# A block of activations split in two halves, modulation sums dealt to other places, and first loads asked for earlier in a two-layer denoising network on one core

## Chip, core and metric

The kernel runs on one core of a Trainium2 chip. The metric is the device time of one execution in microseconds (us). The engines are called by the names of the profile: PE (TensorE, matmuls; PEld is its weight load), DVE (VectorE), ACT (ScalarE), POOL (GpSimd) and SP (SyncE, which here only issues DMAs).

## What is computed

Two layers work on a latent stream of 256 tokens and a context stream of 256 tokens, D = 1024 features each. A layer is a gated FFN, a mixer (layer 0: a short convolution; layer 1: attention) and a second FFN. Each is entered through a modulated norm and left through a modulated gate. The shift, the scale and the gate of each are modulations: nine vectors of 1024 per layer, a product of a conditioning vector with a 1024 x 9216 matrix.

```python
mod  = (silu(c) @ mod_w[i] + mod_b[i]).reshape(bsz, 3, 3, 1, D_MODEL)
modc = (silu(c_ctx) @ mod_w[i] + mod_b[i]).reshape(3, 3, D_MODEL)
lat = lat + 0.5 * mod[:, 0, 2] * _swiglu(_modulate(lat, norm_g[i, 0], mod[:, 0, 0], mod[:, 0, 1]), ffn_w13[i, 0], ffn_w2[i, 0])
cx  = cx  + 0.5 * modc[0, 2] * _swiglu(_modulate(cx, norm_g[i, 0], modc[0, 0], modc[0, 1]), ffn_w13[i, 0], ffn_w2[i, 0])
h, hc = _modulate(lat, norm_g[i, 1], ...), _modulate(cx, norm_g[i, 1], ...)
y, yc = mixer(h, hc)                       # convolution in layer 0, attention in layer 1
lat = lat + mod[:, 1, 2] * y
cx  = cx + modc[1, 2] * yc                 # layer 0 only, as the context's second FFN
...
lat = lat + 0.5 * mod[:, 2, 2] * _swiglu(_modulate(lat, norm_g[i, 2], ...), ffn_w13[i, 1], ffn_w2[i, 1])
```

## The kernel before

**Layout.** Activations lie with features on the 128 partitions and tokens in columns: x is 8 blocks (KT) of 128 features by 512 columns, the latent stream (s = 0) in the first 256 columns and the context (s = 1) in the last 256.

**Precision.** Every matmul operand is split into a high and a low part in fp32r, and three products stand for one (lines 136 to 138). `split` is an ACT copy into the high part (line 107) and a DVE subtraction for the low part (line 108). Weights are split on the fly: a raw tile `wr` is loaded by SP (`load_raw`, line 103; 8 buffers), then split into `wh` and `wl`.

**Stages.** The opening (to 44 us), whose order is written out by hand, then the first FFN of layer 0 (44 to 391), the convolution with its output projection (to 566), the second FFN (to 918), the first FFN of layer 1 (to 1249), attention with its output projection (to about 1360), the last FFN. An FFN runs in three thirds of 8, 7 and 7 blocks of hidden features. A third is a row of pairs (the up and the gate weights of a block) followed by a projection back to the 1024 features (`project`).

**Pairs.** Both streams together are treated as a 2 x 2 block product in seven products instead of eight: half of the features by stream on the one side, the weights' halves on the other. `Pair` loads the raws of a pair (r2, then the right half of r1), POOL scales the left half of r2 by -1 (line 709) and adds the rest by an accumulating DMA (line 712), DVE takes further sums (lines 731 and 739), and `head`, `five`, `six`, `seven` and `four` are the products with their evacuations; `head` copies p and `five` copies q (line 762, tile gm) out of PSUM on ACT.

**Norms.** `tail_norm` collects squares at the end of a projection. The last two output blocks are computed for the latent stream first, then for the context, so that the latent's norm is under way while the context's part is still multiplied. `Blocks.block` forms a block of four feature blocks of a stream: t = x * scale * 1/rms on DVE (line 299), then t + shift. For the latent stream (`fine`) each 256 columns go into bh (ACT, line 391) and bl (DVE, line 392) at once and also into a raw `hr`; for the context the four go into `hr` (ACT, line 396) and are then split as one piece of 1024 columns. `Blocks.sums` then forms the sums of the blocks that the pairs need (`hr` lines 417 to 424). There are three such norms: before the convolution (about 372 to 391), before the second FFN (545 to 566) and before layer 1 (895 to 918).

**Modulation sums.** All modulations but the first two are computed on DVE, one sum (`mod_unit`, line 177) for each tile of 128 x 1024 of the transposed matrix and each stream, 224 sums in all. Their raws `modT` go through the same 8 buffers of `wr` and SP's queue as the weights, and one is always loaded ahead. `tick(n)` adds n to an account and does as many whole sums as it then holds; `project` calls it after its first output blocks with `ev`, `ffn` after each pair with 0.9, the convolution with 0.5. The tuple given to `ffn` holds the `ev` of the first two thirds' projections and that of the last. Where a norm or a gate needs a modulation that isn't done (`mod_ready`, `gate_of`), the missing sums are done on the spot:

```python
    def mod_ready(l, ch):
        while not ((l, ch) in done and done[l, ch] == 8 * streams(l, ch)):
            next_unit()
        return modv[l, ch]
```

**The opening.** The first two modulations are sums on PE (`mod_pe`, line 945) over tiles `pm` that SP loads (line 932) behind the four chunks of x (512 KB, two feature blocks each). `first_sums` squares x by chunks; a one-column copy from x into a pm tile (line 995) makes the loads of pm wait until that chunk of x has landed.

Of the kernel before, what the change touches and what calls it, by code (L numbers as in the profile page):

```python
# [9 lines left out]
F32 = mybir.dt.float32  # L10
# [10 lines left out]
T2 = 2 * S  # L21
# [27 lines left out]
def hybrid_kernel(ctx: ExitStack, tc: tile.TileContext, a: dict, out: bass.AP):  # L49
    nc = tc.nc  # L50
# [55 lines left out]
    def split(hi, lo, src):  # L106
        nc.scalar.activation(out=hi, in_=src, func=AF.Copy)  # L107
        return nc.vector.tensor_tensor(out=lo, in0=src, in1=hi.bitcast(F32), op=ALU.subtract)  # L108
# [105 lines left out]
    def tick(n, at=None):  # L214

        place[:] = [at] if at else []
        owed[0] += n
        while (jobs or units) and owed[0] >= 1:
            owed[0] -= 1
            next_unit()  # L220
        place.clear()
# [93 lines left out]
    def hot(s, dt=F32R):  # L315
        return hop.tile([P, 1024], dt, name=nm(s), tag="hop")
# [56 lines left out]
    class Blocks:  # L373
# [5 lines left out]
        def block(self, s, hf, A, B, ri, fine=False, ks=range(4)):  # L379
            if ks[0] == 0:  # L380
                self.raw[hf, s] = hot("hr", F32)
                self.t["B", hf, s] = hot("bh"), hot("bl")
            raw = self.raw[hf, s]
            hi, lo = self.t["B", hf, s]
            for i in ks:
                k = 4 * hf + i
                c = slice(i * S, i * S + S)
                t = scaled(s, k, A, ri)
                b = B[:, k, s : s + 1]
                if fine:  # L390
                    nc.scalar.activation(out=hi[:, c], in_=t, func=AF.Identity, bias=b)
                    nc.vector.scalar_tensor_tensor(
                        out=lo[:, c], in0=t, scalar=b, in1=hi[:, c].bitcast(F32),
                        op0=ALU.add, op1=ALU.subtract,
                    )
                nc.scalar.activation(out=raw[:, c], in_=t, func=AF.Identity, bias=b)
            if not fine:
                split(hi, lo, raw)

        def at(self, k, c0, c1):  # L400
            return self.blk(("B", k // 4, c0 // S), k % 4)
# [411 lines left out]
    def ffn(l, b, h, tot, gate, tail, gs=(), ev=(0, 0), z=None):  # L813
        gs = list(gs)
        i0 = 0
        for t, n in enumerate(THIRDS):
            between = ()
            if tot == T2:
                heads = []
                if t == 0 and not gs:  # L820

                    gs = [new_pair("g") for _ in range(2)]
                    heads.append(opening(
                        h, [a["w13"][l, b, 0], a["w13"][l, b, 1], lambda: Pair(a["w13"][l, b, 2], h)],
                        lambda pp, i: w13_post(pp, gs[i], 0, T2),
                    ))
                prev = None
                for i in range(len(gs), n):
                    if t == 0 and not heads and i in AS_IS[l, b]:
                        w = load_w(a["w13"][l, b, i])  # L830
                        pp = psum("pg"), psum("pu")
                        if prev:
                            prev.seven()
                        if "T1" not in h.t:
                            with tc.issue_after(rows["W1"]):
                                h.sums()
                        w13_mm(pp, w, h, range(4), 0, T2)
                        if prev:
                            gs.append(new_pair("g"))
                            prev.four(gs[-1])  # L840
                            prev = None
                        w13_mm(pp, w, h, range(4, KT), 0, T2)
                        gs.append(new_pair("g"))
                        tick(3, w13_post(pp, gs[-1], 0, T2))
                        continue
                    if heads:
                        pr = heads.pop(0)
                    else:
                        pr = Pair(a["w13"][l, b, i0 + i], h)
                        pr.sums(0)  # L850
                        pr.sums(1)
                        pr.head()
                    pr.five()
                    at = prev.seven().ins if prev else None
                    pr.six()
                    if prev:
                        gs.append(new_pair("g"))
                        prev.four(gs[-1])
                    prev = pr
                    if i:  # L860
                        tick(0.9, at)

                def last():
                    gs.append(new_pair("g"))
                    prev.four(gs[-1])

                between = (prev.seven, last) if prev else ()
            else:
                for i in range(n):
                    w = load_w(a["w13"][l, b, i0 + i])  # L870
                    gs.append(beside(gp.tile([P, T2], F32R, name=nm("gx"), tag="gh")))
                    pp = psum("pg"), psum("pu")
                    if i0 + i < EARLY:
                        for k in range(KT):
                            for j in range(2):
                                ps = pp[j][:, : z.w]
                                mm3(ps, w(at13(1 - j, k)), z.at(k), k == 0, k == KT - 1)
                            if i == 0 and k == KT // 2:
                                flush(1)
                        if i < 3:  # L880
                            flush(1)
                        early_post(pp, gs[i], z.ri)
                        tick(1)
                        continue
                    for j in range(2):
                        ws = [w(at13(1 - j, k)) for k in range(KT)]
                        mm_wide(pp[j], ws, [h.both(k) for k in range(KT)], True, True)
                    beside_post(pp, gs[i])
                    tick(1)
# [78 lines left out]
    def first_sums():  # L968

        pq = psmall("ss")  # L970
        sq = []

        def square(k, eng):
            tag = "gm" if k % 4 < 2 else "sg"
            t = tp.tile([P, T2], F32, name=nm("sq"), tag=tag, bufs=3)
            if eng is nc.vector:
                nc.vector.tensor_tensor(out=t, in0=x[:, k, :], in1=x[:, k, :], op=ALU.mult)
            else:
                nc.scalar.activation(out=t, in_=x[:, k, :], func=AF.Square)
            sq.append(t)  # L980

        def add():
            a, b = sq[-2:]
            nc.vector.tensor_tensor(out=a, in0=a, in1=b, op=ALU.add)
            n = len(sq)
            for i in range(4):
                nc.tensor.matmul(
                    pq[:, i * P : i * P + P], a[:, i * P : i * P + P], ones,
                    start=(n, i) == (2, 0), stop=(n, i) == (KT, 3), skip_group_check=True,
                )  # L990

        square(0, nc.scalar)
        square(1, nc.vector)
        rows[1, 0] = [hot("pm", F32) for _ in range(2)]
        nc.vector.tensor_copy(rows[1, 0][0][:, :1], x[:, 2, :1])
        add()
        square(2, nc.scalar)
        square(3, nc.scalar)
        add()
        nc.scalar.activation(out=sccol[:, :, 2:4], in_=ccol, func=AF.Silu)  # L1000
        square(4, nc.scalar)
        square(5, nc.vector)
        add()
        square(6, nc.scalar)
        square(7, nc.scalar)
        add()
        nc.vector.tensor_scalar(
            out=sb1, in0=modb[:, 0, KT : 2 * KT], scalar1=1.0, scalar2=None, op0=ALU.add
        )
        return pq  # L1010
# [145 lines left out]


    hn = Blocks()
    ffn(0, 0, h, T2, gate_of(0, 0), tail_norm(0, 1, hn), gs0, (4, 3.4))
    h = hn  # L1160

    zs, ds = [], {}
# [52 lines left out]
    for n in range(2, len(parts)):  # L1215
        if n == 2:
            pr = opening(h, [a["cw_cx"][0], a["cw_cx"][1], parts[2]], conv_post)
        else:
            pr = parts[n]()
            pr.sums(0)  # L1220
            pr.sums(1)
            pr.head()
        pr.five()
        at = prev.seven().ins if prev else None
        pr.six()
        if prev:
            prev.four(None)
        prev = pr
        tick(0.5, at)
    between = (prev.seven, lambda: prev.four(None))  # L1230

    def by_pairs(key, box=None):
# [10 lines left out]
    def ws_out(m):  # L1243
# [3 lines left out]
    hn = Blocks()  # L1247
    project(
        ws_out, lambda k, c0, c1: (zs[k][0][:, c0:c1], zs[k][1][:, c0:c1]), KT,
        gate_of(0, 1), tail_norm(0, 2, hn), T2, 2, 4, between,  # L1250
    )
    h = hn
    hn = Blocks()
    ffn(0, 1, h, T2, gate_of(0, 2), tail_norm(1, 0, hn), (), (3.6, 3))
    h = hn


    hn = Plain()
    ffn(1, 0, h, T2, gate_of(1, 0), tail_norm(1, 1, hn), (), (2.8, 2.2))
    h = hn  # L1260
    ap = ctx.enter_context(tc.tile_pool(name="ap", bufs=2))

# [347 lines left out]
```

## Time and profile before

| | us |
|---|---|
| median of 3 runs | 1549.24 (1548.73 to 1550.27) |
| profiled execution | 1548.97 |
| its span | 1547.2 |
| PE busy | 1533.5 |
| DVE busy | 1298.2 |
| ACT busy | 852.2 |
| POOL busy | 301.3 |

The span runs from the first to the last instruction of the profile; the execution's time lies 1.8 us above it. A line of the profile names the source line, the engine, the operation and the tiles by the program's names (out <- in, buffer numbers left out). The time of L107 and L108 is that of all callers of `split`; the tile says which.

### The profile page before, as it was taken

To read this page: it belongs to the slowest core of one execution; us is meant where nothing else is said; L and a number is where in the kernel's file an instruction comes from. 1 tells how busy PE (TensorE), PEld (TensorE's weight loads), DVE (VectorE), ACT (ScalarE), POOL (GpSimd) and SP (SyncE) were. 2 spreads that over 40 slices of the span, in tenths; PEclk is the share of its full clock that TensorE was granted. 3 is DMA by queue.
4 is the path that set the end of the run, shared out by engine and by line. 5 is a ranking of instruction groups with operands and counts; after the bars stand their busy time and mean duration, and the time that the engine had idled before them with its cause. 6 is when DMAs were issued, how large, how long until landed. Compare 5 with 4: busy or idle time off the path is not lost.

```text
span 1547.2 us, 27333 instructions
## 1 busy us (share of the span) xinstructions
PE 1533.5 (99%) x10594; PEld 1423.6 (92%) x10594; DVE 1298.2 (84%) x1964; ACT 852.2 (55%) x1468; POOL 301.3 (19%) x265
## 2 busy tenths in 40 slices
PE   8999999999999999999999999999999999999999
PEld 6898998999999899989999899989999899998888
DVE  5888788898989999968979889958968788998676
ACT  5644554645655376446456466446456456774553
POOL 0013313402231023042052112043042002300000
PEclk9999999999999999999999999999999999999999
DMA  9568768765356636695796625785697743476562
GB/s 377 199 188 235 162 184 232 164 194 143 75 143 175 206 91 151 212 216 135 213 214 153 207 68 136 220 189 138 210 220 182 253 159 114 142 246 220 170 195 76
DMA packets 97474, 278.80 MB, mean 180 GB/s; under 512 B 11456, under 2 KB 13120, under 8 KB 97344
## 3 DMA queue, kind: packets, MB, share of 16 engines
q1 hardware_dynamic: 69408, 228.10, 45.4%
q0 software_dynamic: 25920, 47.20, 18.1%
q10 hardware_dynamic: 2016, 1.76, 0.4%
q8 instruction: 83, 1.36, 0.4%
q14 instruction: 47, 0.39, 0.1%
HBM read 262.07 MB, written 1.05 MB: 170 GB/s over the span
## 4 chain that ended last, share of the span: by engine, by line
PE 89%; DVE 6%; DMA 2%; ACT 1%; issue 1%; POOL 0%; SPq 0%; DVEq 0%; POOLq 0%; ACTq 0%
PE p L138 8%; PE p L137 8%; PE p L136 8%; PE py L137 8%; PE py L136 8%; PE py L138 8%; PE q L138 6%; PE q L136 6%; PE q L137 6%; PE py L144 2%; PE pu L144 2%; PE pg L144 2%; DVE wl L108 1%; DMA wr<-in_w 1%; PE py L146 1%
## 5 line engine op out<-in xcount | busy, mean ns | idle before, releaser
L107 ACT ACTIVATE wh<-wr 128x1024 fp32r<-128x1024 f32 (+2 forms) x454 | 400.5, 909 | 289.2 <-PE py L137 94.5
L108 DVE TENSOR_TENSOR wl<-wr,wh 128x1024 fp32r<-128x1024 f32 (+2 forms) x454 | 468.6, 1056 | 107.0 <-ACT wh L107 87.0
L177 DVE CUSTOM_DVE_ANT_0 junk<-wr,scbc,first 128x1024 bf16<-128x1024 f32 x209 | 269.9, 1291 | 2.2 <-DMA wr<-in_modT 0.2
L137 PE MATMUL py<-gl,wh 128*128 128x512 f32 (+1 forms) x570 | 213.4, 374 | 0.0
L136 PE MATMUL py<-gh,wh 128*128 128x512 f32 (+1 forms) x570 | 213.4, 374 | 0.0
L138 PE MATMUL py<-gh,wl 128*128 128x512 f32 (+1 forms) x570 | 212.8, 373 | 0.0
L709 POOL TENSOR_SCALAR wr<-wr 128x512 f32<-128x512 f32 x66 | 125.4, 1900 | 424.0 <-DMA wr<-in_w 162.7
L136 PE MATMUL p<-th,wh 128*128 128x256 f32 x528 | 149.5, 283 | 0.0
L138 PE MATMUL p<-th,wl 128*128 128x256 f32 x528 | 149.4, 283 | 0.0
L137 PE MATMUL p<-tl,wh 128*128 128x256 f32 x528 | 149.4, 283 | 0.0
L138 PEld LDWEIGHTS py<-gh,wl 128*128 128x128 f32 x570 | 107.3, 188 | 19.1
L136 PEld LDWEIGHTS py<-gh,wh 128*128 128x128 f32 x570 | 107.4, 188 | 18.3
L137 PEld LDWEIGHTS py<-gl,wh 128*128 128x128 f32 x570 | 107.4, 188 | 18.2
L138 PE MATMUL q<-bh,wl 128*128 128x256 f32 x400 | 113.2, 283 | 0.0
L137 PE MATMUL q<-bl,wh 128*128 128x256 f32 x400 | 113.2, 283 | 0.0
L136 PE MATMUL q<-bh,wh 128*128 128x256 f32 x400 | 113.2, 283 | 0.0
L136 PEld LDWEIGHTS p<-th,wh 128*128 128x128 f32 x528 | 101.3, 192 | 0.4
L137 PEld LDWEIGHTS p<-tl,wh 128*128 128x128 f32 x528 | 101.3, 192 | 0.4
L138 PEld LDWEIGHTS p<-th,wl 128*128 128x128 f32 x528 | 101.3, 192 | 0.0
L114 POOL DMA_DIRECT2D w4l<-in_w x56 | 53.2, 949 | 229.9 <-ACT w4l L113 183.5
L566 POOL DMA_DIRECT2D x<-yg x48 | 44.7, 995 | 215.7 <-ACT yg L563 172.4
L772 ACT ACTIVATE sg<-sg 128x512 f32<-128x512 f32 x56 | 35.3, 631 | 89.0 <-DVE sg L768 88.9
(321 smaller groups left out, 4199.4 us busy)
## 6 DMA issues: line engine op xcount, KB each, us to landing
wr<-in_w SPq DMA_DIRECT2D x120, 512.0 KB, 4.8
wr<-in_modT SPq DMA_DIRECT2D x113, 512.0 KB, 5.1
wr<-in_w2b SPq DMA_DIRECT2D x64, 448.0 KB, 4.0
wr<-in_w2a SPq DMA_DIRECT2D x32, 512.0 KB, 4.4
wr<-in_w SPq DMA_DIRECT2D x56, 256.0 KB, 4.6
wr<-in_w POOLq DMA_DIRECT2D x56, 256.0 KB, 6.0
w4l<-in_w POOLq DMA_DIRECT2D x56, 256.0 KB, 5.8
x<-yg POOLq DMA_DIRECT2D x48, 256.0 KB, 7.6
```

The source lines that it names most:

```text
L107: nc.scalar.activation(out=hi, in_=src, func=AF.Copy)
L108: return nc.vector.tensor_tensor(out=lo, in0=src, in1=hi.bitcast(F32), op=ALU.subtract)
L114: nc.gpsimd.dma_start(out=lo, in_=src, accum_op=ALU.add)
L136: nc.tensor.matmul(ps, wh, mh, start=first, stop=False, **kw)
L137: nc.tensor.matmul(ps, wh, ml, start=False, stop=False, **kw)
L138: return nc.tensor.matmul(ps, wl, mh, start=False, stop=last, **kw).ins
L144: nc.tensor.matmul(ps, w[0], m[2], start=first and n == 0, stop=False)
L146: nc.tensor.matmul(ps[:, :S], w[1], m[0], start=False, stop=last and n == len(ms) - 1)
L177: nc.vector.tensor_tensor_reduce(out=junk, in0=raw, in1=scbc[:, v, :], scale=0.5 if ch in (2, 8) else 1.0, scalar=modb[:, l, col : col + 1 ...
L566: nc.gpsimd.dma_start(out=x[:, m, :], in_=t, accum_op=ALU.add)
L709: nc.gpsimd.tensor_scalar(out=r1[:, :T2], in0=r2[:, :T2], scalar1=-1.0, scalar2=None, op0=ALU.mult)
L772: nc.scalar.activation(out=self.sg, in_=self.sg, func=AF.Silu)
```

## The change

It does three things. The context's block is split in two pieces of 512 columns, each as soon as its two feature blocks are there, instead of in one piece of 1024. The rates of the modulation sums become others: in the first FFN 4.4, 3.8 and 1.3 (after each pair) in place of 4, 3.4 and 0.9; in the convolution 0.4 in place of 0.5 and in its output projection 3 in place of 4; the second FFN's stay; in the first FFN of layer 1 they are 3, 2.5 and 1 in place of 2.8, 2.2 and 0.9. And the one-column copy ahead of the pm loads reads the first chunk of x instead of the second, and stands in front of the square of that chunk.

```diff
@@ class Blocks, block
                 nc.scalar.activation(out=raw[:, c], in_=t, func=AF.Identity, bias=b)
-            if not fine:
-                split(hi, lo, raw)
+                if not fine and i % 2:
+                    c = slice(c.stop - T2, c.stop)
+                    split(hi[:, c], lo[:, c], raw[:, c])
@@ ffn
                     if i:
-                        tick(0.9, at)
+                        tick(ev[2], at)
@@ first_sums
         square(0, nc.scalar)
+        rows[1, 0] = [hot("pm", F32) for _ in range(2)]
+        nc.vector.tensor_copy(rows[1, 0][0][:, :1], x[:, 1, :1])
         square(1, nc.vector)
-        rows[1, 0] = [hot("pm", F32) for _ in range(2)]
-        nc.vector.tensor_copy(rows[1, 0][0][:, :1], x[:, 2, :1])
         add()
@@ the body
-    ffn(0, 0, h, T2, gate_of(0, 0), tail_norm(0, 1, hn), gs0, (4, 3.4))
+    ffn(0, 0, h, T2, gate_of(0, 0), tail_norm(0, 1, hn), gs0, (4.4, 3.8, 1.3))
...
-        tick(0.5, at)
+        tick(0.4, at)
     between = (prev.seven, lambda: prev.four(None))
...
-    gate_of(0, 1), tail_norm(0, 2, hn), T2, 2, 4, between,
+    gate_of(0, 1), tail_norm(0, 2, hn), T2, 2, 3, between,
...
-    ffn(0, 1, h, T2, gate_of(0, 2), tail_norm(1, 0, hn), (), (3.6, 3))
+    ffn(0, 1, h, T2, gate_of(0, 2), tail_norm(1, 0, hn), (), (3.6, 3, 0.9))
...
-    ffn(1, 0, h, T2, gate_of(1, 0), tail_norm(1, 1, hn), (), (2.8, 2.2))
+    ffn(1, 0, h, T2, gate_of(1, 0), tail_norm(1, 1, hn), (), (3, 2.5, 1))
```

## The prediction

> **What bounds the kernel now.** I read the page's busy times first, then what PE (TensorE) waited for, then stretches of time, then the chain of waits at the places where PE stands still.
>
> ```profile
> span 1547.2 us, 27333 instructions
> ...
> PE 1533.5 (99%) x10594; PEld 1423.6 (92%) x10594; DVE 1298.2 (84%) x1964; ACT 852.2 (55%) x1468; POOL 301.3 (19%) x265
> ```
>
> PE is busy for 1533.5 of 1547.2 us: only 13.7 us is there to be won without fewer matmuls, and the change takes no matmul away. So the whole question is which of PE's small holes close and which grow. Its waits, by what ended them (total us, times, longest):
>
> ```profile
> PE pg L136 <- ACT bh L391: 1.4, 1, 1.4
> PE q L136 <- ACT gm L762: 1.2, 1, 1.2
> PE pg L137 <- DVE bl L108: 1.2, 3, 0.4
> PE q L138 <- DVE wl L108: 1.0, 1, 1.0
> ...
> PE ss L269 <- DVE acc L262: 0.5, 2, 0.3
> ...
> PE pr L945 <- DMA pm<-in_mod: 0.5, 1, 0.5
> ```
>
> Each belongs to a place. The three waits for bl are the three norms whose second stream the change splits in halves. The 1.4 for bh is norm 2, before the second FFN of layer 0. The 1.2 for gm is the start of the third third of the first FFN; the 1.0 for wl is just behind norm 1; pm is the opening. The stretches show what stands behind them (start:end length, then busy time and count of PE, PEld, DVE (VectorE), ACT, POOL, then PE's clock, DMA share, GB/s):
>
> ```profile
> 265.00:272.00 7.00, 6.52 (x52) 6.16 (x50) 6.88 (x8) 4.42 (x9) 3.46 (x5) 1.00 1.01 231
> 335.00:377.00 42.00, 42.00 (x238) 36.86 (x237) 36.50 (x61) 18.61 (x29) 8.69 (x6) 1.00 0.68 194
> 391.00:416.00 25.00, 23.57 (x193) 23.14 (x192) 24.39 (x30) 16.16 (x24) 4.89 (x2) 1.00 0.16 39
> 502.00:545.00 43.00, 43.00 (x232) 37.32 (x232) 41.81 (x67) 14.46 (x20) 2.47 (x2) 1.00 0.62 200
> 545.00:566.00 21.00, 19.02 (x153) 18.12 (x151) 20.24 (x44) 14.96 (x33) 7.39 (x7) 1.00 0.65 149
> ...
> 918.00:938.00 20.00, 19.97 (x166) 19.77 (x165) 19.87 (x23) 14.67 (x22) 2.42 (x2) 1.00 0.21 54
> ```
>
> Wherever PE loses time, DVE is full: 6.88 of 7, 24.39 of 25, 20.24 of 21. A modulation sum is DVE work, so moving one moves a hole. One sum, and the splits in both lengths, cost:
>
> ```profile
> L177 DVE CUSTOM_DVE_ANT_0 junk<-wr,scbc,first 128x1024 bf16<-128x1024 f32 x209 | 269.9, 1291 | 2.2 <-DMA wr<-in_modT 0.2
> ...
> L108 DVE TENSOR_TENSOR bl<-hr,bh 128x1024 fp32r<-128x1024 f32 x6 | 7.3, 1219 | 0.0
> ...
> L108 DVE TENSOR_TENSOR tl<-hr,th 128x512 fp32r<-128x512 f32 x8 | 5.2, 687 | 0.0
> ```
>
> **Part 1: modulation weights asked sooner (opening).** The scheduler's placeholder copy moves from the second chunk of x to the first, so the loads of pm that wait for it are issued one chunk earlier.
>
> ```profile
> 6.37 0.33 SPq L932
> ...
> 7.70 7.69 DMA pm<-in_mod
> ...
> 3.00:9.00 6.00, 4.59 (x32) 4.27 (x32) 2.99 (x6) 2.79 (x6) 0.00 (x0) 1.00 1.02 403
> 9.00:11.00 2.00, 1.76 (x14) 1.40 (x13) 1.24 (x3) 1.98 (x3) 0.00 (x0) 1.00 0.88 262
> ```
>
> A chunk of 512 KB at 403 GB/s is 1.30 us, so the first pm load goes out near 5.1 instead of 6.37. Until 9 the DMA engines are full (share 1.02) and an earlier request gains nothing; from 9 to 11 they run at 262 GB/s. Filling that dip is worth 2 x (403 - 262) / 403 = 0.70 us; PE's wait for pm is 0.5. I take -0.5; bounds 0 (the dip has another cause) and -0.7. The Trainium skill ("DMA: Bandwidth & Descriptors", Issuing engines are not separate DMA queues) says that all transfers run on the same 16 engines and interleave whoever starts them; by that an earlier request only shuffles the order of a saturated stretch, and the term would be 0. The row at 9 to 11 is what keeps me from that. SP's queue keeps its order, nothing is moved past anything on it. On DVE the copy now stands ahead of a square, which it delays by one 128x1 copy; the same bounds hold that.
>
> **Part 2: the halves.** Per norm, one 128x1024 subtract of 1219 ns becomes two of 128x512 (687 ns), so DVE pays 155 ns more, and ACT gets two copies for one. In exchange a half is split as soon as its two blocks of 256 columns are there, and both halves now come ahead of the subtraction L417 that stood between them and the norm:
>
> ```profile
> 386.28 2.83 DVE t L299 x7
> 389.11 1.13 DVE hr L417
> 390.25 1.15 DVE bl L108
> ```
>
> The last bl ended at 391.40. In the new order it is 386.28 + 2.83 + 2 x 0.69 = 390.5, 0.9 sooner, and PE needs only the first half to begin. So the 0.4 of each norm goes, with some 0.1 to restart. But hr is not gone, it comes after, and from 391 to 416 DVE is busy 24.39 of 25, from 918 to 938 19.87 of 20: what PE waits for next (wl of the first pair, the 1.0 above) comes no sooner, since the work ahead of it is the same plus 0.155. Of 0.5 I therefore take -0.3 at norm 1 (bounds -0.7 and +0.3, where the later wait grows by the added split and one more) and -0.4 at norm 3, where PE lost only 0.03 us after it (bounds -0.6 and 0).
>
> **Part 3: sums dealt anew.** Counted in the instruction order of both programs, the sums done go from 10 to 11 at the end of the first third's pairs, 30 to 33 after its projection, 37 to 42 and 56 to 63 around the second, 62 to 71 and 72 to 83 around the last, 78 to 88 at the end of the convolution's pairs; before the norm in the tail of the convolution's output projection 9 were forced (87 to 96), and now none is (97 are done by then). Near the attention's output projection 2 were forced and now none is. The total stays 224.
>
> Gain at norm 2. PE's holes there are 1.98 us in 545 to 566 and the last 0.4 for bl just behind. The chain runs over DVE work that a sum precedes:
>
> ```profile
> 545.57 1.19 DVE junk L177
> ...
> 550.62 1.06 ACT wh L107
> 551.68 0.80 ACT bh L391 x2
> ```
>
> Nine sums fewer are 9 x 1.29 = 11.6 us of DVE work out of a stretch where DVE had 1.19 us idle in 43 (502 to 545) and 0.76 in 21. The sum of squares, the copies and bh then come up to a few microseconds sooner, and the 1.98 + 0.4 = 2.4 closes almost wholly; what stays late is the chain of the norm itself (t, bh, bl), some 0.1. I take -2.3, bounds -2.9 (restarts of PE counted) and -1.4 (only the single wait for bh goes). Beside the output projection of the attention I take -0.2, from the 0.5 for acc, which lies half there (bounds -0.3 and 0).
>
> Cost in the first FFN, which takes eleven more sums. Most of it is covered: projections leave DVE 5.5 us idle in 335 to 377, which three more sums (3.9 us) fit into. There I take 0; if a sum falls behind the last square of the norm it costs up to one, +1. Not covered is the start of a third, where the raw weights of the new pair are asked for behind the loads of the sums, in the order of SP's queue, and each load needs a buffer that DVE must free:
>
> ```profile
> 245.56 8.87 DMA wr<-in_w
> ...
> 257.05 5.75 DMA wr<-in_w
> ...
> 270.62 0.70 DVE wr L731
> ...
> 271.39 0.32 ACT wh L107
> ...
> 272.36 0.36 ACT gm L762
> ```
>
> The load asked at 245.56 lands at 254.43, POOL scales it, the accumulating DMA lands at 262.80, and then DVE works without a gap (6.88 of 7) to the sum L731 at 270.62. ACT stands at wh until that has ended, gm is queued behind wh, and PE's q waits 1.2 for gm. The change puts one more sum ahead of it on DVE (1.29 us) and one more 512 KB load ahead of the pair's raws on SP's queue. At the 231 GB/s of this stretch such a load is 2.27 us. If both pass through, gm comes 3.6 us later; if DVE's idle time earlier in the projection takes them up, almost nothing. Bounds +0.4 and +4; I take +2.0, the sum at its full price and a third of the load, since the load is the part that buffers freed sooner can bring back. At the start of the second third the same happens with two more loads, but there the copy gm waits for PE:
>
> ```profile
> L762 ACT COPY gm<-q x2: 374/374/374, 161.3 to 168.5; 128x256 f32<-128x256 f32 x2
> its engine sat idle before it (us, times) until:
>   PE q L138: 0.9, 2
> ```
>
> ACT sat idle before it for 0.9 in two, so there is some cover. I take +0.5, bounds 0 and +2 (two loads, 4.5 us, less what cover the earlier steps have). The other FFNs show no wait of PE at the starts of their thirds, and only the second's rates rise (five more sums over some 350 us, 6.5 us): 0.
>
> **The sum.** -0.5 - 0.3 - 2.3 - 0.4 - 0.2 + 0.5 + 2.0 = -1.2 us. The profiled execution took 1548.97, so 1547.8; the median, 1549.24, lies 0.27 above it, so 1548.0 against the median. A change under 0.2% (3.1 us) is about what a measurement of this kernel can tell from none.
>
> **The rivals.**
>
> *The feed falls behind (slower).* One mechanism, at each start of a third in the first FFN: raws asked for behind added loads in a queue that is already full. At the last third 2.27 + 1.29 = +3.6, at the second two loads less some cover, +2, in the tail +1: +6.6 in place of +2.5. It gives -1.2 + 4.1 = +2.9, 1552.1. It decides from the point where gm at the second third's start is late, since then both starts pay. For it: the 1.01 DMA share and 6.88 of 7 on DVE. Against it: PE's holes there were 1.2 in all, and the projection before it leaves DVE idle. Chance 0.19.
>
> *The idle time absorbs the sums (faster).* The added sums go into DVE's gaps under the projections, gm is no later than before (+0.4, second third 0), and the norms give all of what PE lost: -0.5 - 0.4 - 2.7 - 0.5 - 0.2 + 0.4 = -3.9, 1545.3. For it: 42 of 42 us of PE busy beside 36.50 of DVE in 335 to 377. Against it: DVE is full just where the stall lies. Chance 0.25.
>
> *The halves do nothing.* DVE is the bound after a norm, so a hole closed at bl opens at wl: norms 1 and 3 give 0, the opening 0, norm 2 its 1.4 to 1.9: -1.9 + 2.5 = +0.6, 1549.8. For it: 24.39 of 25. Chance 0.12.
>
> *POOL slows.* The scaling that stands in the chain above could stretch when more sums run beside it:
>
> ```profile
> L709 POOL TENSOR_SCALAR wr<-wr x66: 1481/1830/3990, 73.7 to 1179.4; 128x512 f32<-128x512 f32 x66
>
> ...
> 408.68 3.99 POOL L709 TENSOR_SCALAR wr<-wr 128x512 f32<-128x512 f32 x1 [22.34 <-DMA wr<-in_cw_b]
> ...
> 778.17 1.48 POOL L709 TENSOR_SCALAR wr<-wr 128x512 f32<-128x512 f32 x1 [2.26 <-DMA wr<-in_w]
> ...
> 778.34 1.52 DVE L177 CUSTOM_DVE_ANT_0 junk<-wr,scbc,first 128x1024 bf16<-128x1024 f32 x1
> ```
>
> From the median to the longest is +2.2 us; at two starts that is -1.2 + 4.3 = +3.1, 1552.3. The GPSIMD Engine Reference of the Trainium skill (Key points) says that GpSimd shares its SBUF interfaces with VectorE, with contention where a VectorE instruction has two SBUF inputs, as a sum has. The trace hardly bears it out: the longest, at 408.68, runs in a stretch without sums, and one that starts at 778.17 takes the least there is, 1.48, with a sum from 778.34 beside it; it is the sum that is longer there, 1.52 against 1.29. Chance 0.04.
>
> **How the numbers follow.** The forecast has 0.40. Faster by over 0.2%: most of the absorbing case (0.22) and the low edge of the forecast (0.06), 0.28. Slower: half of the feed case at or above its value (0.12), POOL (0.02), the forecast's upper edge (0.04), 0.18. The rest, 0.54, is within. The likeliest case alone spans 1546.0 to 1550.0. The range takes in the absorbing case with its own spread, 1544.2, and the feed case short of its worst, 1551.6.
>
> **What would show it.** Right: no sum between 545 and 566, the wait for bh at norm 2 gone, no wait for bl at three norms, the first pm load issued near 5.1, and PE's wait for gm at the last third's start grown from 1.2 to some 3. Wrong: that wait unchanged or gone (then the absorbing case), a new wait for gm or wh near 160 (the feed case), the wait for wl behind norm 1 grown by what bl lost (the halves do nothing), or pm landing as late as before.

## The result

The changed kernel takes 1555.81 us (median of 6 runs, 1553.94 to 1559.5), the kernel before 1549.56 beside it: a ratio of 1.004, with an interval of 1.003 to 1.0051. It is slower by some 6 us; the forecast was 1548.0, with 1551.6 as the upper end. The profiled execution took 1558.22, 2.4 us more than its median, and that of the kernel before 0.6 less than the median beside it: the 9.3 us between the two traces stand for 6.2 between the medians.

The page of the changed kernel, and what PE waited for in it (total, times, longest):

```profile
span 1556.4 us, 27333 instructions
...
PE 1536.1 (99%) x10594; PEld 1427.2 (92%) x10594; DVE 1294.6 (83%) x1970; ACT 847.7 (54%) x1474; POOL 300.3 (19%) x265
```

```profile
PE p L136 <- ACT sg L757: 4.9, 2, 4.0
PE q L138 <- DVE wl L108: 3.0, 3, 2.1
PE ss L988 <- DVE sq L985: 2.2, 4, 1.0
PE ss L269 <- DVE acc L262: 1.6, 2, 1.2
PE q L136 <- ACT wh L107: 1.1, 1, 1.1
...
PE q L136 <- ACT gm L763: 1.0, 1, 1.0
```

The waits for bh and bl are gone, and so is the one for pm. In their place stand a wait of 4.0 for sg, which was not there, and one of 2.1 for wl. Both traces hold the same 10594 matmuls, in the same order but for short stretches, mostly at the norms (336 places). So the starts can be compared to a few tenths of a microsecond, and the difference shows where the time went (us by which the changed kernel is behind):

| place | gained or lost there | behind after it |
|---|---|---|
| opening | 0.0 | 0.0 |
| start of the second third, first FFN | +3.6 | 3.6 |
| start of the last third, first FFN | +6.9 | 10.5 |
| before norm 1 (wait for acc) | +0.5 | 11.0 |
| norm 1 and the first pair behind it | -1.3 | 9.7 |
| norm 2 | -3.0 | 6.7 |
| norm 3 | +1.6 | 8.3 |
| start of the last third, layer 1's first FFN | +1.6 | 9.9 |
| attention's output projection and the end | -0.6 | 9.3 |

At the start of the last third the chain of waits of the changed kernel reads (start, length):

```profile
272.13 1.27 DVE junk L177
273.48 0.99 issue
274.47 1.28 DVE junk L177
275.83 0.98 issue
276.81 1.27 DVE junk L177
278.08 0.29 issue
278.50 0.72 ACT yg L564 x2
279.23 0.52 ACT wh L107
279.75 0.27 ACT sg L757
280.06 0.58 PE p L136
```

Three sums stand in it, one behind the other. What lies ahead of them is seen in SP's queue and on DVE (start, length, engine, line, idle time ahead and what ended it), first in the changed kernel, then on DVE in the kernel before:

```profile
252.12 0.36 SPq L103 DMA_DIRECT2D wr<-in_w  x1
```

```profile
271.51 0.69 DVE L732 TENSOR_TENSOR wr<-wr 128x512 f32<-128x512 f32 x1 [4.17 <-DMA wr<-in_w]
272.12 1.28 DVE L177 CUSTOM_DVE_ANT_0 junk<-wr,scbc,first 128x1024 bf16<-128x1024 f32 x1
...
273.33 1.23 DVE L108 TENSOR_TENSOR wl<-wr,wh 128x1024 fp32r<-128x1024 f32 x1
274.47 1.28 DVE L177 CUSTOM_DVE_ANT_0 junk<-wr,scbc,first 128x1024 bf16<-128x1024 f32 x1
...
275.68 1.22 DVE L740 TENSOR_TENSOR wr<-wr,wr 128x1024 f32<-128x1024 f32 x1
```

```profile
262.82 0.69 DVE L731 TENSOR_TENSOR wr<-wr 128x512 f32<-128x512 f32 x1 [1.52 <-DMA wr<-in_w]
263.43 1.28 DVE L177 CUSTOM_DVE_ANT_0 junk<-wr,scbc,first 128x1024 bf16<-128x1024 f32 x1
...
264.64 1.22 DVE L739 TENSOR_TENSOR wr<-wr,wr 128x1024 f32<-128x1024 f32 x1
```

The raws of the pair are asked for at 252.12 where it was 245.56, that is 6.6 us later, of which PE itself is 3.7 behind by then: 2.9 too late. The first sum (line 732, before 731) starts at 271.51 where it was 262.82, 5.0 too late after the same 3.7 are taken off. DVE stands idle for 4.17 us just ahead of it, for the accumulating DMA has not landed: here the load is short and not DVE's time. And the order on DVE is another one: before, one modulation sum stood between that sum and the next (line 739, at 264.64); now two and a subtraction do, so that line 740 starts 11.0 us after the old time of 739, 7.4 too late. ACT's copy sg is queued behind the copies wh that wait for it, and PE's products p behind that.

The hole has a second price, which the clock shows (busy time of the engines, then granted clock, DMA share, GB/s):

```profile
276.00:280.00 4.00, 0.07 (x1) 0.69 0.93 235
280.00:282.00 2.00, 1.94 (x9) 0.50 0.86 161
282.00:284.00 2.00, 2.00 (x11) 0.50 0.68 135
284.00:286.00 2.00, 2.00 (x17) 0.91 1.07 263
...
906.00:908.00 2.00, 2.00 (x12) 0.50 0.00 0
```

PE comes back at half its clock for some 4 us. A matmul of 256 columns starts every 0.21 us there, in place of every 0.12, so the 20 of them take 1.9 us more. Some 0.8 of that would have been lost anyway: at full clock PE would have come by 281.50 to the product that starts at 282.79, but it needs gm, as in the kernel before, and gm's copy ends at 282.31. At norm 3, behind a wait of 1.2 us, PE runs at half again, and some 15 matmuls take 1.3 more. So by this estimate the clock has 2 to 3 of the 9.3 us, as part of the lines of the table above. The six executions go the same way, if roughly: the mean granted clock is 0.999 in that of 1553.94 us and 0.996 in that of 1559.5.

### The profile page after: what moved, and what is told of

Read it like the earlier page. It is cut to its first block, busy times and chain, and to the rows that moved or that the text cites. A ratio compares the mean times of both kernels' runs of the same rounds, so it can differ in the third digit from the quotient of the medians.

```text
span 1556.4 us, 27333 instructions
## 1 busy us (share of the span) xinstructions
PE 1536.1 (99%) x10594; PEld 1427.2 (92%) x10594; DVE 1294.6 (83%) x1970; ACT 847.7 (54%) x1474; POOL 300.3 (19%) x265
## 4 chain that ended last, share of the span: by engine, by line
PE 85%; DVE 6%; DMA 4%; issue 2%; ACT 2%; POOL 0%; SPq 0%; DVEq 0%; POOLq 0%; ACTq 0%
PE p L138 8%; PE p L136 8%; PE p L137 8%; PE py L137 7%; PE py L136 7%; PE py L138 7%; PE q L138 6%; PE q L136 6%; PE q L137 6%; PE py L144 2%; DMA wr<-in_w 2%; PE pu L144 2%; PE pg L144 2%; DVE junk L177 2%; DVE wl L108 1%
## 5 line engine op out<-in xcount | busy, mean ns | idle before, releaser
L177 DVE CUSTOM_DVE_ANT_0 junk<-wr,scbc,first 128x1024 bf16<-128x1024 f32 x214 | 277.2, 1295 | 2.0
L740 DVE TENSOR_TENSOR wr<-wr,wr 128x1024 f32<-128x1024 f32 x66 | 81.5, 1234 | 7.0 <-ACT w4h L112 5.5
```

Of the source, the lines that this page charges most:

```text
L177: nc.vector.tensor_tensor_reduce(out=junk, in0=raw, in1=scbc[:, v, :], scale=0.5 if ch in (2, 8) else 1.0, scalar=modb[:, l, col : col + 1 ...
L740: tt(out=v(r2), in0=v(r2), in1=s2.unsqueeze(1).to_broadcast([P, 2, T2]), op=ALU.subtract,)
```

## The experiments

**Each part alone.** Four kernels, each the kernel before with one part of the change. The edits are those of the diff, so they aren't repeated.

> The kernel before with the halves alone; rates and pm loads as before. Theory (the starts of the thirds in the first FFN lose the time, the halves gain): the waits of 0.4 us for bl at the three norms go, 0.7 us each with the restart, of which norms 1 and 3 give some back; -1 to -2 us, about 1547.8. Rival (the halves cost): two instructions for one on a full DVE make the first pair behind each norm later; 0 to +1.5 us.

Measured: 1547.22 us beside 1550.19 before; 0.9983, interval 0.9974 to 0.9991. PE's waits there:

```profile
PE pg L136 <- ACT bh L391: 1.4, 1, 1.4
PE q L136 <- ACT gm L763: 1.4, 1, 1.4
...
PE p L138 <- DVE wl L108: 0.6, 1, 0.6
```

The three waits for bl are gone, and so is the wait of 1.0 for wl behind norm 1; another of 0.6, on an earlier product, is new. The product that had waited, and the wl it needs, before and with the halves:

```profile
414.76 1.23 DVE L108 TENSOR_TENSOR wl<-wr,wh 128x1024 fp32r<-128x1024 f32 x1
416.04 0.38 PE L138 MATMUL q<-th,wl 128*128 128x256 f32 x1 [1.05 <-DVE wl L108]
```

```profile
414.56 1.21 DVE L108 TENSOR_TENSOR wl<-wr,wh 128x1024 fp32r<-128x1024 f32 x1
416.08 0.28 PE L138 MATMUL q<-th,wl 128*128 128x256 f32 x1
```

So wl comes only 0.2 us sooner. The order of PE's products has changed along with the halves: nine products with w4h, 1.1 us of work, now stand between this product and those ahead of it, and cover the wait. Matched by matmul, PE is 0.2 us behind ahead of norm 1 and 1.1 ahead behind the first pair after it; it gains 0.8 more at norm 2 and 0.5 at norm 3. The sum of -2.6 us lies somewhat beyond the -1 to -2 expected.

> The kernel before with the earlier loads of pm alone. Theory: PE's wait for pm goes but the products behind it wait for the next load (first weights) as before: 0, within 0.3 us. The prediction's term: -0.5 us (0 to -0.7). Rival: the copy ahead of the square delays the sums of squares: +0.2 us or more.

Measured: 1549.68; 0.9999, 0.9991 to 1.0008: nothing that can be told from noise, with room for up to 1.4 us either way. The trace of the changed kernel shows what happens (SP's first loads of pm; the stretches of the opening; PE's products with pm):

```profile
5.16 1.75 SPq L933 DMA_DIRECT2D pm<-in_mod  x4
```

```profile
3.00:9.00 6.00, 4.59 (x32) 4.21 (x32) 2.83 (x5) 2.52 (x5) 0.00 (x0) 1.00 0.97 359
9.00:11.00 2.00, 1.48 (x11) 1.10 (x10) 1.12 (x2) 1.59 (x3) 0.00 (x0) 1.00 0.98 385
```

```profile
14.13 1.93 PE L946 MATMUL pr<-pm,sccol 128*32 128x256 f32 x32
```

The loads start at 5.16 as forecast and the dip from 9 to 11 is filled, 385 GB/s in place of 262. But from 3 to 9 only 359 are moved instead of 403, x lands later, and PE waits 2.2 us for the squares of x where it was 1.6. From 3 to 11 both kernels move the same, some 2.9 MB. The products with pm run without a hole and start 0.7 later, and end at the same time as before. In the trace of this run they end 0.4 us sooner than before (3 to 9: 367 GB/s, 9 to 11: 399), so a gain of that size isn't excluded. The same trace shows how far two traces can differ: PE loses 1.6 us at the last third's start, where this kernel is the kernel before.

> The kernel before with the three rates of the first FFN alone (4.4, 3.8, 1.3). Theory: this is the whole loss: +3.5 us at the second third's start, +6 to 7 at the last third's, with PE's clock at half for some 4 us behind the longest hole, less 2 to 3 us at norm 2, where nothing is forced any more; +6 to +9 us, about 1557. The prediction's sizes: +2.5 - 2.3 = +0.2 us. Rival (the loss is in the other rates or an accident of the profiled run): within 2 us of before.

Measured: 1559.18; 1.0055, 1.0043 to 1.0067, which is +8.5 us. This part is the loss. Its trace has the same wait for sg (4.0 in all) and one of 2.5 us for acc at norm 3, and PE's three waits for bl.

> The kernel before with the other rates alone (convolution 0.4, its output projection 3, first FFN of layer 1 at 3, 2.5 and 1). More sums are then forced at norm 2, 9 to 11. Theory: +0.5 to +2 us, from the start of the last third in layer 1's first FFN (1.5 us in the changed kernel) and norm 2. The prediction had 0 for layer 1. Rival (these rates carry the loss): +4 us or more.

Measured: 1550.8; 1.0, 0.9992 to 1.0009: nothing that can be told from noise. Its trace shows PE 2.3 us further behind from the start of the last third of layer 1's first FFN on; the runs as a whole show no loss of that size, and leave room for one of 1.4 us. The four parts add up: -2.6 + 0 + 8.5 + 0 = +5.9 us, beside +6.2 for the whole change.

**Loads or sums?** Both kernels are the changed one with a part of the sums' work left out in the first FFN, the loads in one, most of each sum in the other.

```diff
@@ load_mod (e5_noload)
+        if probe:
+            return scbc[:, 0, :]
@@ mod_unit (e6_light)
-            in0=raw, in1=scbc[:, v, :],
+            in0=raw[:, :64], in1=scbc[:, v, :64],
```

> The changed kernel, but the sums of the first FFN read a tile that is already there, so that their loads of modulation weights, and their hold on the eight buffers, are left out (the modulations summed there come out other). DVE's work stays. Theory A (the raws of a pair are asked too late, because the sums' loads stand ahead of them and hold the buffers): the holes at the starts of the second and the last third go, and the half clock with them; -8 to -11 us against the changed kernel, about 1546. Theory B (the sums themselves, 1.28 us each on DVE between the steps of the pair, hold up the chain): the holes keep most of their length, -1 to -3 us.

> The changed kernel, but the sums of the first FFN take 64 columns instead of 1024, some 0.13 us in place of 1.28; all loads stay, and what is left out is the rest of each sum. Theory A (late raws): buffers come free a little sooner, the loads still stand in line; at least half of the holes stays, -2 to -5 us against the changed kernel. Theory B (sums on DVE in the chain): the holes go, -8 to -11 us, about 1546.

Measured: 1544.37 without the loads (0.9968, 0.9956 to 0.998) and 1544.71 with the light sums (0.9972, 0.9963 to 0.9982), both some 11 us below the changed kernel. Neither theory in its plain form stands: leaving out either takes the holes at the thirds' starts away (with the light sums one of 1.7 us opens before norm 1, with 3.41 us of half clock). Without loads, DVE still does each sum at its full length:

```profile
257.50 0.68 DVE L735 TENSOR_TENSOR wr<-wr 128x512 f32<-128x512 f32 x1
258.11 1.27 DVE L180 CUSTOM_DVE_ANT_0 junk<-scbc,first 128x1024 bf16<-128x1024 f32 x1
...
259.31 1.21 DVE L743 TENSOR_TENSOR wr<-wr,wr 128x1024 f32<-128x1024 f32 x1
```

but the pair's raws were asked for at 220.73 already, where it is 252.12 in the changed kernel. With the light sums all loads are there, and the raws are asked for at 235.84:

```profile
235.84 0.33 SPq L103 DMA_DIRECT2D wr<-in_w  x1
```

What the two have in common is that early request, and with it an early first sum: 257.50 and 255.40, where it is 271.51. (They share another thing: a single step of DVE stands between the pair's two sums in either, as in the kernel before, where it is three in the changed one.) By the program, a tile of the sums holds one of the eight raw buffers until DVE has done with it, and the pair's load waits for a buffer, so that the load and the sum's time on DVE would act through the same request. This fits both runs but isn't shown by itself; a ninth buffer would test it, and no run has one.

**Where can the sums go?** First behind the pairs instead of into the projections.

```diff
# e7_pairs, on the kernel before
-    ffn(0, 0, ..., gs0, (4, 3.4))           # 0.9 behind each pair
+    ffn(0, 0, ..., gs0, (4, 3.4, 1.3))
# n1_pairs_halves, on the changed kernel
-    ffn(0, 0, ..., gs0, (4.4, 3.8, 1.3))
+    ffn(0, 0, ..., gs0, (4, 3.4, 1.7))      # and 0.5, 4, (2.8, 2.2, 0.9) as before
```

> The kernel before with the rate behind the pairs of the first FFN alone raised (4, 3.4, 1.3). Five or six sums more by the end of the last third, 4 fewer forced at norm 2. Theory (the projections' rates make the holes, since their sums lie ahead of the next third's raws): the starts of the thirds as before, 0 to -1 us. Rival (sums anywhere in the first FFN delay the next raws): +2 to +5 us.

> Halves and earlier pm loads with the dealing (4, 3.4, 1.7), 0.5, 4 and the rest as before: the eleven sums that norm 2 lacked go behind the pairs, and none into the projections. Theory: the halves' -2.6 us and some -2 at norm 2, thirds' starts as before: about 1545.5. Rival (pairs have no room either): holes at the thirds' starts like in the changed kernel, 1550 or more.

Measured: 1552.55 (1.0023, 1.0014 to 1.0031) and 1550.62 (1.0009, 1.0 to 1.0018). The rivals had the sizes right, but the first kernel's loss lies elsewhere than its rival had it. There the hole at the last third's start even shrank, to 0.6 (PE came there 1.2 us later than before), but PE waits for acc at norm 2:

```profile
PE ss L269 <- DVE acc L262: 3.0, 2, 2.6
```

The second has the hole of 4.0 for sg at the last third's start again, with the order on DVE that the changed kernel has, and another of 1.2 for acc before norm 1; the halves' 2.6 us are spent on them. The request alone does not explain its hole: the raws are asked for at 247.44 there and at 248.01 in the first kernel, which has no such hole. But the first sum starts at 265.79 where the first kernel's starts at 263.51, and line 740 at 269.96 where line 739 starts at 265.32.

The next has the halves and the earlier pm loads too, and puts four or so more sums only behind the last third's pairs (1.6 in place of 0.9), where no start of a third follows.

> Halves and earlier pm loads, the dealing of the kernel before, with 1.6 in place of 0.9 behind the pairs of the last third of the first FFN alone, behind which no start of a third comes any more. Four sums fewer are forced at norm 2. Theory: no new hole before norm 1; -2.6 us and up to -1 at norm 2: 1546 to 1547. Rival (fewer forced sums only move the hole there, as in the run with 1.3 behind all pairs, where PE waited 2.8 us for acc): 1548 to 1551.

Measured: 1556.47; 1.0035, 1.0022 to 1.0048, slower than either theory had it, with waits for acc of 3.6 us at norm 2 and 3.1 at norm 3. The chain at norm 3 shows what acc stands behind:

```profile
887.82 7.76 DMA wr<-in_w
895.58 0.02 issue
895.61 0.03 ACT w4h L112
895.63 0.51 issue
896.14 0.62 ACT sq L260
896.76 0.02 issue
896.79 0.69 DVE acc L262
...
900.14 0.90 PE ss L269 x4
```

ACT stands at w4h, a copy for the next stage's first pair, whose load was asked for at 887.82 and lands at 895.58; the norm's square sq is queued behind it on ACT. It is a chain of the same kind with another victim: a raw that lands late, ACT in order behind it, and PE behind ACT. The changed kernel's loss at norm 3 has the same chain, from a load asked for at 890.26 by way of w4h to acc at 903.52. Why the dealing of 400 us earlier shifts this request stays open. The number of sums done by then isn't it: 158 in the kernel before and in the changed one, 159 here, and 162 in the second of the two kernels above, which has no such wait at norm 3.

**Asking earlier.** The same number of sums in each projection, but more behind its first output blocks.

```diff
@@ project, during the first FFN's first two projections
-            tick(ev)           # behind the first three blocks
+            tick(ev * 1.4)
-                tick(ev)       # behind the fourth and fifth
+                tick(ev * 0.4)
```

> The changed kernel with the sums of the first two projections of the first FFN asked earlier: 1.4 times the rate behind the first three output blocks, 0.4 times behind the fourth and fifth; as many sums and loads by the end of each projection. Theory (what counts is when the raws of the next pair are asked, that is how late in the projection buffers are still held by sums): asked several us sooner, the holes at the starts of the second and last third shrink to less than half; -4 to -9 us against the changed kernel, 1547 to 1552. Rival (the first FFN as a whole has no room for eleven more sums, wherever they are put): within 2 us of the changed kernel.

Measured: 1550.39; 0.9999, 0.999 to 1.0008, 6.3 us less than the changed kernel by the two ratios. The second third's start is nearly whole again (0.4 us lost) and norm 3 too. Yet the pair's first raws go out there when they do in the changed kernel (136.17 and 136.21); what comes sooner is the first sum, here the second line, behind the changed kernel's:

```profile
156.47 0.69 DVE L732 TENSOR_TENSOR wr<-wr 128x512 f32<-128x512 f32 x1 [4.80 <-DMA wr<-in_w]
```

```profile
151.31 0.69 DVE L733 TENSOR_TENSOR wr<-wr 128x512 f32<-128x512 f32 x1 [0.55 <-DMA wr<-in_w]
```

In the changed kernel POOL's scaling of these raws waits until 146.28 for a split (wl) of the projection's weights, whose load was asked for at 133.87 and took 9.96 us; here it starts at 144.13. At the last third's start the raws are asked for at 250.07, with PE hardly behind, so still some 4 us too late, and there the hole of 4.0 for sg stays.

> Halves and earlier pm loads, the dealing of the kernel before, with the sums of the two projections asked earlier in the same way. Theory: -2.6 us from the halves and up to -1.4 from the hole at the last third's start: about 1546. Rival (the hole of 1.4 us has another cause, or the earlier sums make another): 1547 to 1549.

Measured: 1546.04; 0.9972, 0.9961 to 0.9983, 4.3 us below the kernel before and the fastest of those that leave nothing out. The hole that it was to close is still there (1.3 for gm; the raws are asked for at 245.40, as before), so why it would be better than the halves alone is not shown; their intervals overlap.

**The order on DVE.** In the changed kernel, for the first pair of the second and of the last third, line 740's sum is issued ahead of the subtraction for S1 and S2.

```diff
@@ class Pair
+        def sums_first(self):
+            ...
+            tt(out=s2, in0=s2, in1=s1, op=ALU.subtract)
+            ...
+            split_far(*self.w["A22"], r2[:, :T2], ...)
+            tt(out=v(r2), in0=v(r2), in1=s2..., op=ALU.subtract)     # as line 740
+            self.keep(("S1", "S2"), r1)
+            self.keep(("S3", "S4"), r2)
```

> The changed kernel with the steps of the first pair of the second and the last third in another order: DVE's sum for S3 and S4 (line 740) ahead of the subtraction for S1 and S2, as it stood in the kernel before at the last third and no longer stands in the changed one. Loads, sums and their number as in the changed kernel. Theory C (the order adds to the late raws: a subtraction and a sum more, 1.2 + 1.3 us, stand between the two sums, and ACT's copy of PSUM stands behind both): the hole at the last third's start shrinks from 6.3 us by 1.2 to 3; -1.5 to -4 us against the changed kernel. Theory A alone (only the asking of the raws counts): within 0.7 us of it.

> As the last, and the sums of the two projections asked earlier as in the run e8_front. If both causes add up: the hole of 4.2 us that e8_front kept at the last third's start goes to 1 to 2, -2 to -4 us against e8_front, about 1547. Theory A alone: as e8_front, 1550.

Measured: 1553.37 (1.0022, 1.0013 to 1.0031) with the order alone, 2.8 us below the changed kernel by the ratios, whose intervals just touch; with both, 1550.2 (1.0003, 0.9994 to 1.0012), no better than with the earlier sums alone, where 2 to 4 us less were expected. In the trace with the order alone the wait for sg falls from 4.0 to 0.9, and another takes its place:

```profile
PE q L138 <- DVE wl L108: 4.0, 2, 3.1
```

The first sum starts at 269.45 there, and what it feeds is late whichever way the steps behind it are ordered. So the order was worth 2.8 us by itself and nothing on top of the earlier sums.

What PE loses at the last third's start goes rather with how late the first sum starts, each beyond what PE is behind there (one trace each, so good to 1 or 2 us; minus is early, and gained):

| kernel | first sum late | PE loses |
|---|---|---|
| 1.3 behind the pairs | -0.6 | -0.8 |
| 1.7 behind the pairs, with halves | 2.9 | 4.5 |
| earlier sums and the old order | 3.6 | 6.0 |
| earlier sums | 4.1 | 6.7 |
| the old order | 4.4 | 5.3 |
| changed | 5.0 | 6.9 |
| rates of the first FFN alone | 5.3 | 7.9 |

That start takes in the request, the buffers and the time of the DMAs. By these rows raws that are whole late are the main part, which no experiment shows by itself; how much of it each of the three has was not separated.

## Why the prediction was wrong

**What bounds.** PE's holes, each ended by a full DVE: this held in part. Behind the first sum DVE works without a gap, but ahead of it it stands idle for 4.80 us at the second third's start and 4.17 at the last's, waiting for raws. That a hole is also paid in clock was missed.

**Opening, -0.5.** Not borne out: 0 in the changed kernel's trace, 0.4 in that of the loads alone, and nothing that the runs can tell from noise. The dip was filled, which was forecast, but at the price of x. The rule that was set aside would have given 0: by the Trainium skill ("DMA: Bandwidth & Descriptors", Issuing engines are not separate DMA queues) transfers interleave on the same engines whoever starts them. The trace agrees with it: the four loads of x land in 5.8 us (median) where it was 5.4, and some 2.9 MB are moved from 3 to 11 us in both kernels.

**Halves, -0.3 and -0.4.** Right in sign, too small. Alone they gain 2.6 us, norm 2 included, whose 0.4 the prediction had put into the next term. That wl comes no sooner was nearly right (0.2 us); the step that failed is that PE's order was taken as it stood, so that the wait of 1.0 would stay.

**Norm 2, -2.3.** Right: -3.0 in the trace, of which the halves alone give 0.8; -2.4 in the trace with the rates of the first FFN alone. No sum is between 530 and 560, and PE is busy from 545 to 566 without a hole.

**Starts of the thirds, +0.5 and +2.0.** This is the step that failed, at +3.6 and +6.9; the sign named for it came too, new waits for wl (2.1) and gm (1.0) near 160. The mechanism was named (raws behind the sums' loads, in a queue and in buffers that DVE frees), and the rival that rests on it was named too, with 1552.1 and a chance of 0.19. Three things made the price too small. At the last third one added load and one added sum were priced, the load at a third, on the argument that buffers freed sooner bring it back. In the trace SP asks for 7 tiles of the sums in the projection, ahead of the pair's raws, where it was 5, and DVE does 21 modulation sums from the projection's first product to line 740 where it was 19 to line 739; and the raws were asked for 2.9 us too late, so nothing was brought back. Two of each at the prediction's own full prices, 2 x 2.27 + 2 x 1.29, are 7.1 beside the 6.9 measured, though the half clock is in the 6.9, so that the nearness is in part luck. At the second third the two loads were counted rightly (7 for 5), but the cover that was read off, ACT idle for 0.9 us, did not hold: the first sum starts 5.6 us too late. And the chain was followed to gm alone with its old order; the new dealing also changed the order of DVE's steps and put sg behind them.

**Layer 1, 0.** The changed kernel loses 1.6 us at the last third's start there, for five sums more; the part by itself moved nothing that could be told from noise.

**Norm 3, and the clock.** Neither loss was in the sum: +1.6 at norm 3 in place of -0.4, where a load is asked for late, and 2 to 3 us at half clock in all.

**POOL.** The rival by which scaling would stretch beside sums had 0.04; POOL's busy time is 300.3 us after 301.3, and the scaling of the last third's first pair takes 1.98 where it was 2.04, so it played no part there. One reading under this rival doesn't hold: the longest scaling, at 408.68, has no modulation sum beside it, but DVE does subtractions of two tiles (line 108) all along, which have two SBUF inputs as a sum has. Another, at 453.20, takes 1.49 us beside such subtractions, so the trace leaves open whether they stretch it.

## What to carry to other kernels

Work that is moved to fill idle time of an engine also moves its loads and the buffers that they hold, and the idle time of that engine says nothing about either. Before moving it, look up when the next stage's first load is asked for and what frees its buffer; here the first sum's delay of some 5 us came out whole, behind everything that is queued in order after it. And try the parts of a change alone: here one part was worth having and another cost three times as much.

## What was unexpected of the hardware

PE's granted clock fell to 0.50 behind holes, and in steps: in the changed kernel for 6.83 us at the start of the last third, where PE had 4 us and more without work, and for 3.41 us at norm 3, behind a wait of 1.2 us and the norm's own small products. Waits of 1.2 and 1.4 us that stood by themselves, at the last third's start and at norm 2 in the kernel before, and even one of 2.1 at the second third's start in the changed kernel, left the clock at 1.00. In all other traces with half clock before the kernel's end its length was 3.41 us or two or three times that. The length of the hole doesn't set it alone: a wait of 4.0 us for sg goes with 6.83 us in two traces and with 3.41 in a third. Half clock cost a little under half its length where PE had work (a matmul every 0.21 us in place of 0.12).
